# Expert rows fetched by an indirect transfer per pair, and a context branch paced behind the experts' matmuls

## The chip, the cores and the metric

The kernel runs on one core of a Trainium2 chip. A core has a matrix engine (TensorE, PE in the profile; PEld is its weight load), a vector engine (DVE), an activation engine (ACT), a general engine (POOL) and a queue engine (SP) that here only issues transfers. ACT and POOL can issue transfers too. All transfers share the core's 16 DMA engines. The metric is device time in microseconds (us) of one launch.

## The reference, cut to what matters

Two transformer blocks follow one another on 512 tokens of width 1024, all in float32. The first ends in a mixture of experts where each expert chooses its tokens:

```python
def expert_choice_ffn(h, w_router, w_gate, w_up, w_down):
    cap = EC_FACTOR * N // N_EXPERTS                      # 64 tokens for each of 16 experts
    aff = jax.nn.softmax((h @ w_router).astype(F32), axis=-1)
    gate, idx = lax.top_k(jnp.swapaxes(aff, 1, 2), cap)
    xg = jax.vmap(lambda hb, ib: hb[ib])(h, idx)          # the rows that an expert chose
    hid = jax.nn.silu(einsum(xg, w_gate)) * einsum(xg, w_up)   # 64 x 2048
    y = einsum(hid, w_down) * gate[..., None]
    # y is added back into the rows it came from
```

`h` is the normalised token row times one vector plus another (the modulation). One expert's three weight matrices are 1024 x 2048 float32, 25.2 MB; sixteen are 403 MB, most of what the kernel reads. The second block needs, beside its own token stream, the keys, values and scan states of 256 context rows. These depend on inputs alone, so this context branch can run at any time before the second block's mixer.

## The kernel before, in words

A tile framework orders the instructions of each engine; program order and priorities decide, and semaphores are put in by the framework. Three stages matter here.

The router stage (`g_b0`, `g_b1`) normalises the 512 rows into `xn` (four tiles of 128 rows, L1482, L1484), transposes them, computes the router's scores, and finds each expert's 64 tokens. Its result is `slt` (L1574): for each token and expert the slot from 0 to 63, or a number that is no slot.

The expert stage (`g_b`) goes over 16 experts in pairs. At the start of a pair, `pair` builds a 0/1 matrix `S` (512 tokens by 2 x 64 slots, L1589) on DVE and multiplies: for each of 8 slices of the width, 4 matmuls of 128 x 128 with the strided columns of `xn` as weights pick the chosen rows, already transposed; DVE and ACT then apply the modulation on the way out of the accumulator (L1600, L1598) and write `XG`. The first four slices come before the expert's matmuls, the last four after half of its gate and up weights. POOL multiplies `S` by the router's weights (L1602), and four transposes (L1605) make the scatter matrix `P`.

An expert's weights come as 12 tiles of 2 MB ("weight tiles"): 8 alternating between gate and up, then 4 of down. Each is used by 8 matmuls of 64 x 512, which the profile shows as 16 instructions. After the 8 gate and up tiles ACT and DVE form the hidden rows (L1673, L1674), 8 transposes turn them (L1680), and the down tiles follow. After the second expert of a pair, 8 matmuls of 128 x 512 with `P` add its rows into the accumulator `acc` (L1715 to L1718).

Weight tiles land in rooms of 2 MB, and a load is issued by SP, in order, as soon as its room is free, so the matmuls' use of a tile releases a later load. Four rooms go round in a ring (`wr`); three others (`sum_b`, `out_b`, `in_b`) serve once each at the start, before they get their later use. `out_b` later holds the pair's result rows `Y`, `in_b` holds `XG` of every other pair among others. When the context branch has ended, its room makes three more, and the ring has seven.

The context branch (`g_c0`) is a generator: 24 blocks of weights of `w_in_2` (0.5 MB each, 0.25 MB the first), each multiplied with the 256 context rows in 8 matmuls (16 instructions) into the one accumulator `bank_c`, followed by a short convolution on ACT and DVE, transposes and state products. In the expert stage `weave` interleaves it with the experts by weights: an expert counts 0.12, a block of the branch 0.03, and the branch starts at 0.3. The framework may place its matmuls anywhere between those of the experts. Its loads are issued by ACT.

## Time and profile before

| what | value |
|---|---|
| median of 3 runs | 3045.6 us (3041.74 to 3050.76) |
| the profiled execution | 3043.58 us, its span 3041.8 us |
| PE busy in the span | 2863.8 us (94%) |
| DVE, ACT, POOL busy | 1344.8, 911.3, 632.5 us |
| granted TensorE clock, mean | 0.987 |
| moved by DMA | 652.04 MB, mean 214 GB/s |

The profile cuts the span into 40 slices of 76 us. The expert stage is the stretch where the DMA engines are busiest, from about 730 us to 1776 us. There, a table by stretches shows whether PE, the transfers or both are at their limit, and the chain of waits shows what each stretch hung on. A busy PE isn't necessarily PE at its peak: an instruction that streams behind another counts as busy.

### The profile page before, as it was taken

How to read it: one execution, taken by the hardware profiler on the slowest of the kernel's cores; microseconds unless marked ns; L12 is line 12 of the kernel's file. 1: busy time of each engine (PE TensorE's matmuls, PEld its weight loads, DVE VectorE, ACT ScalarE, POOL GpSimd, SP SyncE). 2: the span in 40 equal slices, each digit the busy share in tenths (PEclk: the TensorE clock that was granted, in tenths of full speed). 3: DMA queues.
4: the chain of work that ended last, by engine and by line, in shares of the span. 5: the costliest groups of instructions: out<-in, count | busy, mean ns of one | idle time of the engine just before them, and what ended most of it. 6: DMA issues, size and time to landing. Idle time of an engine off the chain costs nothing.

```text
span 3041.8 us, 42842 instructions
## 1 busy us (share of the span) xinstructions
PE 2863.8 (94%) x17300; PEld 1885.2 (62%) x17300; DVE 1344.8 (44%) x2673; ACT 911.3 (30%) x1855; POOL 632.5 (21%) x662
## 2 busy tenths in 40 slices
PE   7999999998999999899999989999989999999998
PEld 4894557756354534243343348687868678878886
DVE  5522546654221211011011047969797945364445
ACT  5511226532111010000000034545454543243333
POOL 3121225521000000000000022323232323242232
PEclk9999999999999999999999989999999999999999
DMA  7216661047979897999999953333332375243331
GB/s 263 76 45 199 216 195 34 25 162 289 375 310 386 316 371 317 423 430 431 430 431 431 430 192 103 108 87 102 87 115 74 96 261 166 90 153 97 97 104 56
DMA packets 255430, 652.04 MB, mean 214 GB/s; under 512 B 15672, under 2 KB 168760, under 8 KB 230656
## 3 DMA queue, kind: packets, MB, share of 16 engines
q1 hardware_dynamic: 212368, 600.95, 52.5%
q10 hardware_dynamic: 42864, 48.35, 4.8%
q8 instruction: 136, 2.23, 0.3%
q14 instruction: 62, 0.51, 0.1%
HBM read 627.61 MB, written 21.64 MB: 213 GB/s over the span
## 4 chain that ended last, share of the span: by engine, by line
PE 59%; DVE 9%; DMA 5%; ACT 2%; issue 1%; POOL 1%; POOLq 0%; ACTq 0%; DVEq 0%
PE bank_mm L367 25%; PE bigbank L367 22%; PE bank_pj L367 6%; PE bank_c L367 3%; DMA b<-in_w_down 2%; DVE base L2389 1%; PE bank_sm L367 1%; DMA l<-in_w_up 1%; DMA wo<-in_w_down 1%; DVE mix L2393 1%; DVE mix L2392 1%; DMA l<-in_w_gate 1%; PE bank_mm L2144 1%; DVE c L1927 1%; DVE base L2122 1%
## 5 line engine op out<-in xcount | busy, mean ns | idle before, releaser
L367 PE MATMUL bank_pj<-c,c 128*128 128x512 f32 (+2 forms) x1368 | 318.5, 375 | 0.3 <-DVE c L1927 0.3
L367 PE MATMUL bank_mm<-c,c 128*128 128x512 f32 (+1 forms) x1608 | 305.0, 348 | 2.5 <-DVE c L1927 1.3
L367 PEld LDWEIGHTS bank_mm<-c,c 128*128 128x128 f32 x1608 | 259.9, 191 | 42.1 <-DVE c L1927 1.7
L367 PEld LDWEIGHTS bank_pj<-c,c 128*128 128x128 f32 (+1 forms) x1368 | 224.9, 188 | 50.5 <-issue 17.5
L367 PE MATMUL bank_mm<-l 128*128 128x128 f32 (+3 forms) x944 | 227.4, 496 | 4.2 <-DVE l L395 2.0
L1926 ACT CAST c<-base 128x1024 fp32r<-128x1024 f32 x147 | 153.0, 1045 | 253.8 <-PE bigbank L367 105.7
L1927 POOL TENSOR_TENSOR c<-base,c 128x1024 fp32r<-128x1024 f32 x47 | 115.7, 2462 | 450.4 <-DMA base<-in_w_in 201.4
L367 PEld LDWEIGHTS bank_mm<-l 128*128 128x128 f32 (+2 forms) x944 | 155.3, 245 | 73.9 <-issue 65.2
L367 PE MATMUL bigbank<-l 128*64 128x512 f32 (+1 forms) x864 | 195.9, 587 | 4.5 <-DMA l<-in_w_up 2.4
L1927 DVE TENSOR_TENSOR c<-base,c 128x1024 fp32r<-128x1024 f32 x100 | 135.3, 1355 | 139.1 <-ACT c L1926 135.4
L1674 DVE TENSOR_TENSOR b<-l,bigbank 128x512 f32<-128x512 f32 x32 | 20.6, 684 | 257.8 <-PE bigbank L367 227.8
L367 PEld LDWEIGHTS bigbank<-l 128*64 128x64 f32 (+1 forms) x864 | 61.4, 141 | 117.8 <-issue 104.0
L367 PE MATMUL bank_c<-b 128*128 128x256 f32 (+3 forms) x496 | 117.5, 380 | 12.7 <-ACT b L1841 8.3
L1602 POOL TENSOR_TENSOR l<-l,ab 128x512 f32<-128x512 f32 x8 | 8.4, 1048 | 560.2 <-DVE l L1589 506.6
L367 PE MATMUL bigbank<-out,c 128*128 128x512 f32 x480 | 112.5, 394 | 2.4 <-ACT out L2487 1.8
L367 PEld LDWEIGHTS bank_c<-b 128*128 128x128 f32 (+1 forms) x496 | 79.0, 190 | 54.8 <-issue 30.1
L367 PE MATMUL bank_mm<-h,sp 128*128 128x512 f32 (+3 forms) x544 | 106.9, 384 | 4.6 <-ACT h L606 3.8
L367 PEld LDWEIGHTS bank_dn<-dn 64*64 64x64 f32 x1920 | 74.5, 134 | 55.1 <-issue 40.1
L367 PE MATMUL bigbank<-b,l 128*64 128x512 f32 x480 | 105.7, 593 | 2.1 <-DMA b<-in_w_up 1.2
L367 PEld LDWEIGHTS bigbank<-out,c 128*128 128x128 f32 x480 | 90.9, 190 | 22.9 <-ACT out L2487 2.0
L1598 ACT ACTIVATE l<-bank_mm,ab,ab 128x128 f32<-128x128 f32 x32 | 14.7, 458 | 293.0 <-DVE l L1600 292.9
L367 PE MATMUL bigbank<-c,ffn 128*128 128x512 f32 x432 | 100.4, 390 | 0.0
(556 smaller groups left out, 5096.1 us busy)
## 6 DMA issues: line engine op xcount, KB each, us to landing
l<-in_w_up SPq DMA_DIRECT2D x25, 2048.0 KB, 10.7
l<-in_w_gate SPq DMA_DIRECT2D x25, 2048.0 KB, 9.4
l<-in_w_down SPq DMA_DIRECT2D x25, 2048.0 KB, 16.2
base<-in_w_in SPq DMA_DIRECT2D x90, 512.0 KB, 3.7
mods<-in_w_mod SPq DMA_DIRECT2D x80, 512.0 KB, 4.7
base<-in_w_up SPq DMA_DIRECT2D x18, 2048.0 KB, 8.7
wo<-in_w_gate SPq DMA_DIRECT2D x18, 2048.0 KB, 10.2
b<-in_w_gate SPq DMA_DIRECT2D x15, 2048.0 KB, 19.5
```

The costliest lines, as they stand in the source:

```text
L367: self.mm_ins = self.nc.tensor.matmul(out, l, r, start=start, stop=stop).ins
L1598: nc.scalar.activation(XG[:, kt], b[:, kk], AF.Identity, bias=b2[:, kt:kt + 1], scale=a2[:, kt:kt + 1])
L1602: nc.gpsimd.tensor_mul(sc, S, aff[:, :, ee, None].to_broadcast([128, 4, 2, 64]))
L1674: nc.vector.tensor_mul(hid[:, 512 * j:512 * j + 512], s, ac[1][:, j])
L1926: nc.scalar.copy(hi, raw)
L1927: (nc.vector if self.wn % 4 in self.losplit else nc.gpsimd).tensor_sub(lo, raw, hi.bitcast(F32))
L2122: nc.vector.tensor_reduce(mx, s[:, s0:768], AX.X, OP.max)
L2144: nc.tensor.transpose(tb[:, z], p[:, 128 * (g0 + z):128 * (g0 + z) + 128], self.ident)
L2389: nc.vector.scalar_tensor_tensor(E[:, h], rw[:, h, 0], gc(1, 0, h), E[:, h], op0=OP.subtract, op1=OP.min)
L2392: nc.vector.tensor_scalar(W[:, h], cb[:, c, 0], gc(0, 0, h), None, op0=OP.mult)
L2393: nc.vector.scalar_tensor_tensor(W[:, h], cb[:, c, 1], gc(0, 1, h), W[:, h], op0=OP.mult, op1=OP.add)
```

## The change

The rows of `xn` are now written to memory (`xnd`, four transfers of 512 KB issued by ACT in the router stage), and a column `tid` holds each token's row number. For each pair, 4 matmuls of `S` with `tid` (128 x 1) give the row numbers of the 128 slots, DVE converts them to integers, and POOL issues one indirect transfer that fetches the 128 rows (512 KB) into `Y`, the buffer in which the pair's results will stand later. Eight transposes of `Y` then take the place of the 32 matmuls. The modulation and `P` are as before.

The order changes too. The first pair is fetched and transposed before its matmuls. Every later pair is prepared in the odd expert ahead of it: fetch at its start, transposes after its hidden rows, and then the multiplication for `P`. The addition into `acc` is put off into the next expert, half behind its first two weight tiles and half behind its next two.

The room of `xn` becomes a fifth room of the ring (eight after the context branch), and `out_b` no longer serves as a weight room at the start.

The context branch starts at 0.1 instead of 0.3, its steps count 1.7 times as much, an expert's weight is handed out in smaller steps, and each step's PE instructions are ordered behind the last expert matmul issued so far (`issue_after`, which orders instructions on one engine and makes no semaphore). It asks for its weight blocks one block earlier.

```diff
+def paced(K, gen, f):
+    while True:
+        with K.tc.issue_after(K.ex_ins):
+            v = next(gen, None)
+        if v is None:
+            return
+        yield v * f
...
+C0_LATE, C0_PACE = 0.1, 1.7
...
+        z, self.tid = self.small()[:, :1], Part(self.s1b, 144, [4]).ap()
+        nc.vector.tensor_reduce(z, self.km("gt"), AX.X, OP.add)
+        nc.vector.tensor_scalar(self.tid, self.col("iota64", 0, 4), 128.0, z, op0=OP.mult, op1=OP.add)
+        self.xnd = self.dram_tile([512, 1024], "xnorm")
+        for t in range(4):
+            nc.scalar.dma_start(self.xnd[128 * t:128 * t + 128], xn[:, t])
...
-    def pair(self, pr):
+    def pair(self, pr, Y):
...
+        b = self.bank((128, 1))
+        for t in range(4):
+            self.mm(b, S[:, t].rearrange("p e s -> p (e s)"), self.tid[:, t:t + 1], t == 0, t == 3)
+        ix = self.ix[:, pr:pr + 1]
+        nc.vector.tensor_copy(ix, b)
+        nc.gpsimd.indirect_dma_start(Y, None, self.xnd, bass.IndirectOffsetOnAxis(ix, 0))
+        yield
         for k4 in range(2):
             b = self.bank((128, 4, 128))
             for kk in range(4):
-                for t in range(4):
-                    self.mm(b[:, kk], xn[:, t, 4 * k4 + kk::8], S[:, t].rearrange("p e s -> p (e s)"), t == 0, t == 3)
+                nc.tensor.transpose(b[:, kk], Y[:, 4 * k4 + kk::8], self.ident)
...
     def g_b(self, experts=range(16)):
+        self.xn_b.free()
...
-        wr.b += [self.slot(), self.wo_b]
-        more = [None, None, sum_b.ap(), out_b.ap(), None, None, in_b.ap()]
+        wr.b += [self.slot(), self.wo_b, Buf(M, [4096])]
+        more = [None, None, sum_b.ap(), None, None, None, in_b.ap()]
...
+            if e == ex[0]:
+                begun = self.pair(e // 2, yr())
+                next(begun)
+                next(begun)
+            if e % 2 == 0:
+                XG, P, Y = self.nxt
...
-            if e % 2 == 0:
-                Y = yr()
-                prep = self.pair(e // 2)
+            if e % 2 and e != ex[-1]:
+                prep = self.pair(e // 2 + 1, yr())
                 next(prep)
...
+                self.ex_ins = self.mm_ins
+                if owed:
+                    owed.pop(0)()
+                yield 0.018
...
+            with self.tc.issue_after(self.ex_ins):
+                next(prep, None)
+            yield 0.006
...
+                owed += [lambda add=add: add((0, 1)), lambda add=add: add((2, 3))]
+            yield 0.024
...
-            w = wr()
-            self.c0_ld(w, w2[:, :, K0 + 128 * c:K0 + 128 * c + 128])
+            w = block()
...
-            weave(self.g_b(), late(0.3, c0))
+            weave(self.g_b(), late(C0_LATE, paced(self, c0, C0_PACE)))
```

In the rows of the order that follow, `x4` behind a row counts like instructions of the program in a row (a matmul counts once there and as two instructions in the profile). `bigbank` is the accumulator of gate and up, `bank_mm` that of everything else of the experts, `bank_c` that of the context branch; `l_105`, `b_6410`, `base_95` and `wo_6154` are pools of memory, `ab_126` holds the small constants, `base_59` the identity.

PE at the start of the first pair, before:

```order
L1572 MATMUL bank_mm<-base_59,l_105 128x16 x4
L367 MATMUL bank_mm<-l_105 128x128 x19
L367 MATMUL bigbank<-l_105 64x512 x16
L367 MATMUL bigbank<-b_6410,l_105 64x512 x16
L367 MATMUL bank_mm<-l_105 128x128 x13
L367 MATMUL bank_c_7244<-b_6410 128x256 x2
L367 MATMUL bigbank<-base_95,l_105 64x512 x8
```

The same place in the changed kernel:

```order
L1590 MATMUL bank_mm<-base_59,l_105 128x16 x4
L377 MATMUL bank_mm<-ab_126,l_105 128x1 x4
L1618 MATMUL bank_mm<-base_59,b_6410 128x128 x8
L377 MATMUL bigbank<-l_105 64x512 x16
L377 MATMUL bigbank<-b_6410,l_105 64x512 x8
L377 MATMUL bigbank<-base_95,l_105 64x512 x8
L377 MATMUL bigbank<-wo_6154,l_105 64x512 x8
L377 MATMUL bigbank<-l_105 64x512 x24
L1630 MATMUL bank_mm<-base_59,l_105 128x128 x4
L1718 MATMUL bank_mm<-base_59,b_6410 128x128 x8
```

The 19 and 13 picking matmuls are gone. The row numbers (128x1) and the transposes of the fetched rows (L1618) stand one behind the other, with nothing of the context branch between them.

PE from the second to the third expert, where the second pair starts, before:

```order
L367 MATMUL bank_mm<-l_105 64x512 x8
L367 MATMUL bank_c_7543<-b_6410 128x256 x2
L367 MATMUL bank_mm<-b_6410 128x512 x8
L367 MATMUL bank_mm<-l_105 128x128 x19
L367 MATMUL bigbank<-l_105 64x512 x8
```

In the changed kernel the second pair is prepared inside the second expert. Its row numbers, at that expert's start:

```order
L377 MATMUL bank_c_6899<-b_6410 128x256 x8
L377 MATMUL bank_mm<-ab_126,l_105 128x1 x4
L377 MATMUL bigbank<-l_105 64x512 x3
L1899 MATMUL bank_c_6913<-base_59,b_6410 128x128 x2
L377 MATMUL bigbank<-l_105 64x512 x13
L377 MATMUL bigbank<-base_95,l_105 64x512 x8
L377 MATMUL bigbank<-wo_6154,l_105 64x512 x8
L377 MATMUL bank_c_6968<-b_6410 128x256 x8
```

and the transposes of its rows, behind the eighth weight tile:

```order
L377 MATMUL bigbank<-l_105 64x512 x19
L377 MATMUL bigbank<-base_95,l_105 64x512 x8
L1618 MATMUL bank_mm<-base_59,b_6410 128x128 x8
L1718 MATMUL bank_mm<-base_59,b_6410 128x128 x8
L377 MATMUL bank_mm<-wo_6154,l_105 64x512 x8
```

Between the row numbers and the transposes stand the 64 matmuls of eight weight tiles and one block of the context branch; in every later pair it is eleven tiles. A block of the branch is now 8 matmuls in one piece. In the whole stage 19 blocks are left for the expert pairs in both kernels: before, all of them stand in the first three pairs; now 3, 5, 5, 4 and 2 of them in the first five.

POOL from the first pair on, before (L1602 makes `P`'s factor, L1846 and L1857 belong to the context branch):

```order
L1602 TENSOR_TENSOR l_105<-l_105,ab_126 128x512 x2
L1846 TENSOR_TENSOR b_6410<-b_6410 128x512 x2
L1602 TENSOR_TENSOR l_105<-l_105,ab_126 128x512
L1846 TENSOR_TENSOR b_6410<-b_6410 128x512
L1857 TENSOR_TENSOR b_6410<-b_6410 128x512
```

and in the changed kernel (L1613 is the fetch, L1626 and L1905 are L1602 and L1846 of before):

```order
L1613 DMA b_6410<-xnorm,ab_126 128x1024
L1626 TENSOR_TENSOR l_105<-l_105,ab_126 128x512 x2
L1613 DMA b_6410<-xnorm,ab_126 128x1024
L1626 TENSOR_TENSOR l_105<-l_105,ab_126 128x512
L1905 TENSOR_TENSOR b_6410<-b_6410 128x512 x2
L1613 DMA b_6410<-xnorm,ab_126 128x1024
```

The fetches stand in POOL's queue between the multiplications of the context branch, so from the third on a fetch is issued only after those ahead of it.

## Rows read from the trace of the kernel before

**Rows 1.** Page, slices of the whole span: mean GB/s in each of 40.

```profile
GB/s 263 76 45 199 216 195 34 25 162 289 375 310 386 316 371 317 423 430 431 430 431 431 430 192 103 108 87 102 87 115 74 96 261 166 90 153 97 97 104 56
```

**Rows 2.** Chain of waits, pairs' starts and the stage's end: start us, us, what.

```profile
729.99 9.49 PE bank_mm L367 x38
...
868.89 15.78 PE bank_mm L367 x54
...
1026.77 15.78 PE bank_mm L367 x54
...
1180.31 16.04 PE bank_mm L367 x54
...
1306.81 16.05 PE bank_mm L367 x54
...
1776.17 4.66 DMA base<-in_w_in
```

**Rows 3.** Stretches by pair: us, engines' busy us, PEclk, DMA share, GB/s.

```profile
730.00:870.00 140.00, 132.83 (x589) 65.38 (x590) 25.86 (x68) 19.98 (x41) 4.14 (x4) 0.97 0.88 351
870.00:1027.00 157.00, 149.39 (x631) 70.88 (x630) 28.75 (x55) 19.35 (x39) 11.30 (x11) 1.00 0.90 350
1027.00:1180.00 153.00, 145.51 (x608) 67.24 (x606) 24.90 (x47) 16.35 (x34) 13.34 (x13) 0.99 0.86 334
...
1307.00:1424.00 117.00, 109.36 (x485) 47.74 (x485) 15.69 (x28) 5.17 (x10) 1.05 (x1) 1.00 1.01 431
```

**Rows 4.** The same stretches, instructions on the context branch's accumulator alone.

```profile
730.00:870.00 140.00, 29.47 (x118) 20.03 (x118) 5.97 (x14) 5.89 (x17) 0.97 0.88 351
870.00:1027.00 157.00, 41.66 (x148) 24.71 (x148) 10.46 (x20) 9.92 (x20) 1.00 0.90 350
1027.00:1180.00 153.00, 35.60 (x124) 20.59 (x124) 8.53 (x16) 8.42 (x17) 0.99 0.86 334
```

**Rows 5.** Groups by form, 1310 to 1430 us: busy us, mean ns, idle before.

```profile
L367 PE MATMUL bank_mm<-l 128*128 128x128 f32 x64 | 15.5, 401 | 0.0
...
L1598 ACT ACTIVATE l<-bank_mm,ab,ab 128x128 f32<-128x128 f32 x4 | 1.8, 458 | 53.7 <-DVE l L1600 53.7
L1600 DVE TENSOR_SCALAR l<-bank_mm,ab,ab 128x128 f32<-128x128 f32 x4 | 1.6, 407 | 7.5 <-PE bank_mm L367 7.0 <-ACT l L1598 0.5
...
L1605 PE MATMUL bank_mm<-base,l 128*128 128x128 f32 x4 | 0.6, 272 | 0.0
```

**Rows 6.** Chain of waits in a later pair, around one expert's hidden rows.

```profile
1343.63 10.54 PE bigbank L367 x48
...
1360.42 13.95 PE bank_mm L367 x64
1374.37 17.19 PE bigbank L367 x80
```

**Rows 7.** Instructions by time at the first pair: start us, us, engine, idle before.

```profile
729.54 0.29 DVE L1589 TENSOR_TENSOR l<-ab,ab 128x128 f32<-128x128 f32 x1
...
730.74 0.49 DVE L1589 TENSOR_TENSOR l<-ab,ab 128x128 f32<-128x128 f32 x2
...
739.40 7.09 PE L367 MATMUL bigbank<-l 128*64 128x512 f32 x32
...
743.10 0.33 SPq L398 DMA_DIRECT2D l<-in_w_up  x1
...
753.29 6.46 PE L367 MATMUL bank_mm<-l 128*128 128x128 f32 x26
...
764.03 3.60 PE L367 MATMUL bigbank<-wo,l 128*64 128x512 f32 x16
```

**Rows 8.** Transfers of the context branch's blocks (512 KB), 680 to 1200 us.

```profile
DMA to landing us min/median/max: 3.6/4.6/19.8
```

**Rows 9.** POOL's waits, 740 to 1180 us: us in total, times, longest.

```profile
POOL b L1846 <- ACT b L1841: 119.9, 4, 72.0
```

More of the change, by code (lines that the diff above doesn't have):

```diff
@@ L1600, in pair @@
                     nc.vector.tensor_scalar(XG[:, kt], b[:, kk], a2[:, kt:kt + 1], b2[:, kt:kt + 1], op0=OP.mult, op1=OP.add)
-            yield
+        yield
         nc.gpsimd.tensor_mul(sc, S, aff[:, :, ee, None].to_broadcast([128, 4, 2, 64]))
+        yield
         b = self.bank((128, 4, 128))
@@ L1615, in g_b @@
         self.S = Buf(M, [4, 2, 64]).ap()
+        self.ix = Part(self.s1b, 128, [16]).ap().bitcast(mybir.dt.uint32)
         self.XG_r = R(Buf(M, [8, 128]), Part(in_b, 0, [8, 128]))
@@ L1636, in fetch @@
                 self.ld(w, src)
-        gt2, ex = self.gt2_b.ap(), list(experts)
+        gt2, ex, owed = self.gt2_b.ap(), list(experts), []
         self.fg_b = self.gt1_b
         for e in experts:
-            if not self.c0 and len(wr.b) < 7:
+            if not self.c0 and len(wr.b) < 8:
                 p = wr.i % len(wr.b)
@@ L1657, in g_b @@
             for q in range(4):
-                if q == 2:
-                    next(prep, None)
                 for m, src in enumerate((g, u)):
@@ L1667, in g_b @@
                                 self.mm(ac[m][64 * a:64 * a + 64, j], XG[:, kt, 64 * (e % 2):64 * (e % 2) + 64], w[:, k2, 1024 * a + 512 * j:1024 * a + 512 * j + 512], kt == 0, kt == 7)
-            for _ in prep:
-                pass
+                self.ex_ins = self.mm_ins
+                if owed:
+                    owed.pop(0)()
+                yield 0.018
+            if e == ex[0]:
+                for _ in begun:
+                    pass
             hid = hr()
@@ L1690, in g_b @@
                             self.mm(dn[64 * h:64 * h + 64], hT[:, 4 * q + j, 64 * a:64 * a + 64], w[:, j, 512 * h:512 * h + 512], a + q + j == 0, a == 1 and q == 1 and j == 3)
+                self.ex_ins = self.mm_ins
+                next(prep, None)
+                if a == 0:
+                    yield 0.018
             pp = slice(64 * (e % 2), 64 * (e % 2) + 64)
@@ L1704, in g_b, with add @@
                 self.c_open()
-            if e % 2:
                 for t in range(4):
-                    if e == ex[-1]:
-                        b = on.pop(0) if on else under(t)
-                        for h in range(2):
-                            hs = slice(512 * h, 512 * h + 512)
-                            self.mm(b[:, hs], P[:, 128 * t:128 * t + 128], Y[:, hs], False, True)
-                        self.c_tile(t, b)
-                        continue
-                    for h in range(2):
-                        b = self.bank()
-                        self.mm(b, P[:, 128 * t:128 * t + 128], Y[:, 512 * h:512 * h + 512])
-                        o = acc[:, t, 512 * h:512 * h + 512]
-                        nc.vector.tensor_add(o, o, b)
-            yield 0.12
+                    b = on.pop(0) if on else under(t)
+                    for h in range(2):
+                        hs = slice(512 * h, 512 * h + 512)
+                        self.mm(b[:, hs], P[:, 128 * t:128 * t + 128], Y[:, hs], False, True)
+                    self.c_tile(t, b)
+            elif e % 2:
+                def add(ts, P=P, Y=Y):
+                    for t in ts:
+                        for h in range(2):
+                            b = self.bank()
+                            self.mm(b, P[:, 128 * t:128 * t + 128], Y[:, 512 * h:512 * h + 512])
+                            o = acc[:, t, 512 * h:512 * h + 512]
+                            nc.vector.tensor_add(o, o, b)
+                owed += [lambda add=add: add((0, 1)), lambda add=add: add((2, 3))]
+            yield 0.024
 BF = mybir.dt.bfloat16
@@ L1791, in g_c0, with ask, block @@
         w2 = self.w2()
-        w = wr()
-        self.c0_ld(w[:, :, :64], w2[:, :, DT0:DT0 + 64])
+        cols = [(DT0, 64)] + [(K0 + 128 * c, 128) for c in range(4)]
+        for gr in range(4):
+            cols += [(XS0 + 512 * gr + 128 * i, 128) for i in range(4)] + [(BM0 + 128 * gr, 128)]
+        asked = []
+        def ask():
+            if cols:
+                o, n = cols.pop(0)
+                asked.append(wr())
+                self.c0_ld(asked[-1][:, :, :n], w2[:, :, o:o + n])
+        def block():
+            ask()
+            return asked.pop(0)
+        ask()
+        w = block()
         b = self.bank((128, 256), "c0")
@@ L1800, in g_c0 @@
         for c in range(4):
-            w = wr()
-            self.c0_ld(w, w2[:, :, K0 + 128 * c:K0 + 128 * c + 128])
+            w = block()
             for t in range(2):
@@ L1866, in g_c0 @@
                 ch = (XS0 + 512 * gr + 128 * i) if i < 4 else (BM0 + 128 * gr)
-                w = wr()
-                self.c0_ld(w, w2[:, :, ch:ch + 128])
+                w = block()
                 b = self.bank((128, 256), "c0")
```

5 lines of the change are left out of this document (2 added, 3 removed).

## Prediction

> **What bounds the kernel now.** I read the page's slices first, then the chain of waits inside the expert stage, then the stretches by pair, and last the rows of single steps. The slices show two halves of the stage [rows 1]: from the tenth to the sixteenth slice the transfers move 289 to 386 GB/s, after that 423 to 431 GB/s without a break. The chain gives the pairs' starts [rows 2]: 730.0, 868.9, 1026.8, 1180.3 and 1306.8 us, and the stage's end at 1776.2 us. So the first four pairs take 138.9, 157.9, 153.5 and 126.5 us, and the last four 469.4 us, 117.3 each.
>
> What limits a late pair? Its 24 weight tiles of 2.097 MB are 50.3 MB, which at 431 GB/s [rows 3] is 116.8 us (4.87 us a tile). That is the pair's length: late pairs hang on the transfers. PE is nearly full beside them. By the chain [rows 6] an expert's gate and up matmuls end at 1354.2 us, its down matmuls start at 1360.4 us and end at 1374.4 us, and this first expert of the pair had begun at 1306.8 us: 67.6 us without a wait for a load. The second one, taken without waits, is 8 tiles of 3.6 us [rows 7], the 6.2 us between, and 13.95 us: 49.0 us. Together PE needs 116.6 us, as much as the transfers.
>
> What limits an early pair? PE is busy 132.8 of 140, 149.4 of 157 and 145.5 of 153 us there, and the transfers run at 334 to 351 GB/s [rows 3]. The instructions on the context branch's accumulator hold PE for 29.5, 41.7 and 35.6 us of it [rows 4]. So in the first three pairs the context branch stands on top of a PE that was full already, and the transfers lose what PE is late. The fourth pair (126.5 us) has no branch left but runs on four rooms.
>
> The gain therefore lies in the first four pairs, where PE time counts. In the last four a shorter PE buys nothing.
>
> **The change part by part.** All numbers are us, against the profiled execution (3043.58, of which the span is 3041.8). The median of the runs, 3045.6, is 2.0 more; I subtract the same gain from it.
>
> *Picking matmuls out.* 64 instructions, 15.5 a pair [rows 5]. On the path in pairs one to four; hidden under the transfers later.
>
> *Row numbers, transposes in.* The 4 narrow matmuls are 8 instructions. No row shows this form. The same count of transposes would take 1.2 (0.15 each, 0.6 for four [rows 5]), of picking matmuls 1.9 (0.242 each). I take 1.5, in the middle. The 8 transposes are 1.2. The drains of the transposes to `XG` are as many as before, 4 on ACT at 0.458 and 4 on DVE at 0.407 [rows 5], but they now stand in front of the copies of the turned hidden rows, which the down tiles wait for: 1.6. Sum 4.3 a pair, on the path in the first four pairs (bounds 2.4, with nothing behind the drains, and 4.7). Net 15.5 - 4.3 = 11.2 a pair.
>
> *The fetch.* For later pairs PE has other work between the row numbers and the transposes. In the second pair it is eight tiles and a block of the branch, 8 x 3.6 + 5.6 = 34; in the others eleven tiles, at least 39. A 512 KB transfer lands in 4.6, at most 19.8 [rows 8]. So I cost the wait at nothing there. The first pair has no cover: `S` is complete at 731.2 [rows 7], the row numbers 1.5 later at most, the conversion 0.3 (as the nearest small DVE row, a part of `S`, takes 0.29), landing 4.6, about 2.4 more since a weight tile of 4.87 is under way at that time (half of it), transposes 1.2, first drain 0.4. First expert matmul at 741.6 instead of 739.4 [rows 7]: +2.2. With the landing at 3.6 alone or at 19.8 this is -1 to +15. In return the second half of the old picking, 6.5 at 753.3 [rows 7], goes, and the first half is what the fetch replaces.
>
> DVE is busy 28.8 of 157 us in an early pair, in 55 instructions of 0.5 us [rows 3]; what that does to a transfer that POOL issues, no row shows. The Trainium skill, page "SBUF — State Buffer", section "A bandwidth-pool intuition that's wrong", speaks against such a fetch: POOL writes the descriptors itself and waits while a vector copy holds the port that the two share; it gives 0.62 us for a transfer alone and 3.1 us beside such a copy. By that rule I estimate up to 2.5 us more at the first pair and nothing under the cover, and the sum would come to 2998 or 2999.
>
> *Rows of xn to memory.* Four issues on ACT in front of the drains that feed the router, and two small DVE instructions: no row for their delay in that place; each issue of a transfer on a queue takes some 0.33 [rows 7]. Four are 1.3; I take +1.5 for all (0 to 3).
>
> *The branch spread.* 19 blocks cost 29.5 + 41.7 + 35.6 = 106.8 before, 5.6 each. Now 3, 5, 5, 4 and 2 of them stand in pairs one to five: 16.8, 28, 28, 22.4, 11.2. That changes pairs one to three by -12.7, -13.7 and -7.6, and loads the next two.
>
> *Weight rooms.* Five instead of four while the branch runs, one fewer at the start. Pairs two and three need 24 x 4.87 + 5 x 1.2 + 1.2 = 124 of transfers, PE more than that, so I give the fifth room no gain of its own.
>
> The sum by pairs:
> - first: 138.9 + 2.2 - 6.5 + 4.3 (preparing the second) - 12.7 = 126.2
> - second: 157.9 - 11.2 - 13.7 = 133.0
> - third: 153.5 - 11.2 - 7.6 = 134.7
> - fourth: PE 116.6 - 11.2 + 22.4 = 127.8 (transfers 122.9)
> - fifth: PE 116.6 - 11.2 + 11.2 = 116.6, transfers 116.8 + 2.4 + 1.2 = 120.4; the transfers end last
> - sixth and seventh: 116.8 + 1.2 (the fetch's 0.5 MB) = 118 each; eighth 117.3
>
> Together 995.4 instead of 1046.2: 50.8 less. Minus 1.5 for the stores: 49.3. The profiled execution would take 2994 and the median 2996.
>
> What is late next: PE in the first four pairs, still, and the transfers from the fifth on. Two things I leave at zero, since they pull against each other: rooms that are full when the branch ends give a lead of at most 3 tiles (15 less), and pairs two to four run both limits within 10 us of each other, where each hiccup of one stalls the other (a few us a pair more).
>
> **The rivals.**
>
> *The transfers never idle (2958, chance 0.15).* If blocks fill the 6.2 us pauses at the hidden rows [rows 6], PE keeps up everywhere. From the eighth load at 743.1 [rows 7] there are 185 tiles (900), 19 blocks (23), 4.9 for `acc`, 7 fetches (8.5), 4.9 of states: 941, and a last tile's 3.6, so 1688 instead of 1776.2: 88 less. For it: in the changed order a block stands in the pause of some experts. Against it: PE's sum in pairs two and three is 9 above the transfers'.
>
> *The solid blocks stall PE (3021, chance 0.22).* The branch has one accumulator. Its transposes now come a few expert matmuls behind a block (half a tile, 1.8 us), and must wait until ACT and DVE have drained the block and convolved it: three passes of about 0.5 each [rows 4] and their hand-overs. Where that takes 3 us instead of 1.8, 19 blocks lose 1.3 each: 25 of the 49 are gone. For it: PE executes in order, so an expert's ready matmul stands behind. Against it: DVE and ACT are busy under 20% [rows 3].
>
> *The fetch comes late (3100, chance 0.05; the slower side).* From the third fetch on it stands in POOL's queue behind multiplications of the branch, which waited up to 72 us for their turn before [rows 9]. PE's transposes wait in order, and all expert matmuls and releases of rooms behind them. The cover is 34 in the second pair and about 50 in the next three (11 tiles and two blocks). At 72 us that is 38 + 3 x 22 = 104 against the 49 gained: 55 slower, 3100. It turns from gain to loss at about 58 us. Against it: those multiplications belong to blocks that are earlier in PE's order too.
>
> *Nothing moves (3045, chance 0.06).* The transfers themselves would have to be slow in the first pairs, and not PE late. Their 334 to 351 GB/s beside a PE at 95% speak against it [rows 3].
>
> **How the numbers follow.** My forecast has 0.52, the four rivals 0.15, 0.22, 0.05 and 0.06. The likeliest time is 2996. The unknown terms (start -1 to +15, stores 0 to 3, the drains -2, lead and stalls about 15 to each side) make 2976 to 3019 for it alone. Out to most of the two neighbouring rivals the range is 2964 to 3027. 0.3% is 9 us, about what a measurement here can tell from no change: faster has 0.52 + 0.15 + 0.21 = 0.88 (a little of the second rival falls short), same 0.06 + 0.01 = 0.07, slower 0.05.
>
> **What would show it.** Right: pairs of about 126, 133, 135, 128 and then 117 to 120; no matmul group of 15.5 us at a pair's start; first expert matmul within some us of 742; the branch's last instruction near the end of the fifth pair; transfers near 400 GB/s in pairs two to four. Wrong: PE waiting at L1618 in later pairs (fetch late); PE waiting at L1899 for DVE (solid blocks); transfers at 431 from the second pair on (first rival); pairs six to eight below 116.

## The result and the profile after

| | before | changed |
|---|---|---|
| median | 3048.2 us | 2996.95 us (2990.4 to 3003.8, 4 runs) |
| ratio | 1 | 0.9839 (95%: 0.9806 to 0.9872) |
| profiled execution | 3043.58 us | 2990.43 us, its span 2988.6 us |

One run of the kernel before took 4054 us; the median above counts it, the ratio leaves it out. The forecast was 2996 us. How did it come about, and is it the time that the forecast was made of?

The page's slices of the changed kernel, mean GB/s in each of 40, answer [rows 1]:

```profile
GB/s 268 75 36 198 219 209 30 37 148 278 412 416 414 395 416 412 410 382 431 429 431 431 428 98 102 121 70 128 64 122 68 125 250 158 93 158 93 98 99 57
```

From the eleventh slice on the transfers now move 382 to 416 GB/s, where it was 310 to 386 up to the sixteenth. They still don't reach 431 until the nineteenth slice.

The stretches by pair answer [rows 3]. Columns: stretch, us, busy us (and instructions) of PE, weight loads, DVE, ACT and POOL, granted clock as a share of full speed, DMA share, GB/s.

```profile
727.00:846.00 119.00, 108.02 (x496) 45.24 (x496) 23.72 (x68) 16.51 (x30) 5.34 (x5) 0.96 0.93 383
846.00:976.00 130.00, 122.86 (x527) 49.33 (x528) 21.68 (x45) 15.55 (x34) 7.15 (x7) 0.99 0.99 414
976.00:1109.00 133.00, 124.22 (x534) 49.88 (x533) 23.05 (x46) 12.85 (x27) 8.20 (x8) 1.00 0.98 405
1109.00:1239.00 130.00, 124.69 (x534) 50.10 (x534) 22.74 (x44) 13.42 (x28) 8.20 (x8) 1.00 0.98 405
1239.00:1369.00 130.00, 118.40 (x488) 43.62 (x486) 19.37 (x36) 10.31 (x21) 9.20 (x9) 0.99 0.95 403
1369.00:1487.00 118.00, 99.13 (x438) 33.02 (x436) 15.23 (x28) 4.96 (x10) 2.03 (x2) 1.00 1.01 430
```

The reader is to see two things. PE's time fell in the first three pairs and in the late ones (109 to 99), and rose in the fourth and fifth, which now hold blocks (112 to 125 and 109 to 118); but only the first three pairs became shorter. And in pairs two to four the DMA engines are busy for 0.98 to 0.99 of the time, at 405 to 414 GB/s, while PE has 5 to 9 us of idle time.

A pair's length is taken from the first instruction that weights a pair's last results (DVE, line 1734, before 1692) to the same of the next pair. The first pair counts from the first instruction that picks rows, at 729.99 us before and 727.17 after. All in us:

| pair | 1 | 2 | 3 | 4 | 5 | 6 | 7 | 8 | sum |
|---|---|---|---|---|---|---|---|---|---|
| before | 137.9 | 157.4 | 154.3 | 126.5 | 116.7 | 117.8 | 117.0 | 118.5 | 1046.2 |
| forecast | 126.2 | 133.0 | 134.7 | 127.8 | 120.4 | 118 | 118 | 117.3 | 995.4 |
| changed | 118.5 | 129.9 | 133.4 | 130.5 | 130.0 | 117.9 | 119.2 | 117.8 | 997.2 |

The expert stage gave 49.0 of the 53.2 us between the two profiled executions. Of the rest, 2.8 came before it and 1.3 after it.

The chain of waits from the second to the fourth pair (start us, us, what; the longest of 157 pieces) answers [rows 2]:

```profile
by line: DMA b<-in_w_in 31.0%; PE bigbank L377 23.2%; PE bank_mm L377 17.0%; DMA l<-in_w_up 15.0%; PE bank_c L377 10.8%; DVE b L1709 0.7%; SPq L408 0.6%; ACT l L403 0.6%; PE bank_c L1899 0.6%; PE bank_mm L1718 0.6%; PE bank_mm L1630 0.4%; P
...
838.17 33.96 DMA b<-in_w_in
872.62 13.30 DMA l<-in_w_up
893.37 29.35 DMA b<-in_w_in
923.67 17.03 DMA l<-in_w_up
```

`b<-in_w_in` is a branch's weight block, 512 KB. Its landing takes up to 34 us, where it was 3.6 to 19.8 before [rows 8]; some blocks still land within 3.5 to 10 us. 46% of this chain are transfers. What do they hold up? SP's waits in the same stretch (us in total, times, longest):

```profile
SPq L408 <- PE bigbank L377: 157.8, 39, 9.8
SPq L408 <- DMA b<-in_w_in: 143.7, 8, 20.4
```

Eight times SP, which issues the experts' weights, waits for the landing of a branch's block. It needs nothing of that block, which goes into a room of the branch. Why the program makes it wait isn't in the trace. After one of these waits, at 872 us, SP issues three loads within 3 us.

The first pair by time (start us, us, engine, line, operation, idle before) answers [rows 7]:

```profile
726.73 0.29 DVE L1607 TENSOR_TENSOR l<-ab,ab 128x128 f32<-128x128 f32 x1
...
728.26 0.61 PE L377 MATMUL bank_mm<-ab,l 128*128 128x1 f32 x4 [0.21 <-DVE l L1607]
728.90 0.16 DVE L1612 CAST ab<-bank_mm 128x1 uint32<-128x1 f32 x1 [0.49 <-PE bank_mm L377]
...
729.93 1.21 POOL L1613 DMA_INDIRECT b<-xnorm,ab  x1 [12.05 <-issue]
...
736.66 1.97 PE L1618 MATMUL bank_mm<-base,b 128*128 128x128 f32 x8 [7.79 <-DMA b<-xnorm,ab]
...
738.56 2.79 PE L377 MATMUL bigbank<-l 128*64 128x512 f32 x8
```

And all eight fetches (durations of the POOL instruction in ns, min/median/max; its transfers' landing in us; who waited for line 1613):

```profile
L1613 POOL DMA_INDIRECT b<-xnorm,ab x8: 980/983/1213, 729.9 to 1534.1; - x8
...
  PE bank_mm L1618: 7.8, 1
...
DMA to landing us min/median/max: 6.3/11.0/11.4
```

From `S` to the first expert matmul it takes 11.83 us instead of 9.86. PE waits for a fetch once, in the first pair.

### The profile page after: what moved, and what is told of

It reads as the page before. It is cut to its first block, busy times and chain, and to the rows that moved or that the text cites. A ratio compares the mean times of both kernels' runs of the same rounds, so it can differ in the third digit from the quotient of the medians.

```text
span 2988.6 us, 42066 instructions
## 1 busy us (share of the span) xinstructions
PE 2780.2 (93%) x16916; PEld 1779.9 (60%) x16916; DVE 1342.4 (45%) x2683; ACT 910.4 (30%) x1855; POOL 641.8 (21%) x670
## 4 chain that ended last, share of the span: by engine, by line
PE 46%; DMA 17%; DVE 8%; issue 2%; ACT 1%; POOL 1%; SPq 0%; POOLq 0%; ACTq 0%; DVEq 0%
PE bank_mm L377 18%; PE bigbank L377 17%; DMA l<-in_w_up 7%; PE bank_pj L377 6%; DMA l<-in_w_down 4%; DMA b<-in_w_in 4%; PE bank_c L377 2%; DMA l<-in_w_gate 1%; DVE base L2447 1%; PE bank_sm L377 1%; DVE mix L2451 1%; DVE mix L2450 1%; DVE c L1985 1%; PE bank_mm L2202 1%; DVE base L2180 1%
## 5 line engine op out<-in xcount | busy, mean ns | idle before, releaser
L377 PE MATMUL bigbank<-l 128*64 128x512 f32 (+1 forms) x1104 | 264.0, 593 | 25.4 <-DMA l<-in_w_up 19.1
L377 PEld LDWEIGHTS bigbank<-l 128*64 128x64 f32 (+1 forms) x1104 | 78.2, 140 | 185.4 <-issue 139.8
L1708 ACT ACTIVATE l<-bigbank 128x512 f32<-128x512 f32 x32 | 17.4, 594 | 420.4 <-PE bigbank L377 420.4
L377 PE MATMUL bank_mm<-l 128*64 128x512 f32 (+2 forms) x528 | 125.1, 598 | 11.2 <-DMA l<-in_w_down 9.3
L1803 ACT ACTIVATE b<-bank_c,base 128x256 f32<-128x256 f32 x20 | 11.3, 564 | 307.0 <-PE bank_c L377 307.0
L377 PE MATMUL bigbank<-b,l 128*64 128x512 f32 x352 | 82.5, 607 | 19.8 <-DMA b<-in_w_gate 11.2
L377 PE MATMUL bank_dn<-dn 64*64 64x64 f32 x1920 | 96.2, 225 | 4.2 <-DVE dn L988 1.3
```

Of the source, the lines that this page charges most:

```text
L377: self.mm_ins = self.nc.tensor.matmul(out, l, r, start=start, stop=stop).ins
L1708: nc.scalar.activation(s, ac[0][:, j], AF.Silu)
L1803: nc.scalar.activation(y, b, AF.Identity, scale=wc(1), bias=self.col(bname, i))
```

## The experiments

Two theories were set against each other. T is the prediction: PE bounds pairs one to four. R came from the rows above: the transfers bound pairs two to five, slowed by the branch's loads. Each result is a ratio to the kernel before in the same series (median 3046 to 3048 us), mostly of five runs. The last column is the sum of pairs two to four in the profiled execution, in us (393.8 in the first one of the changed kernel).

| kernel | median us | ratio (95%) | pairs 2 to 4 |
|---|---|---|---|
| changed, again | 2997.7 | 0.9838 (0.9824 to 0.9851) | 399.1 |
| fetch alone | 3010.4 | 0.9872 (0.9856 to 0.9887) | 399.5 |
| spread alone | 3042.6 | 0.9988 (0.9979 to 0.9997) | 420.3 |
| four rooms | 3002.4 | 0.9854 (0.9839 to 0.9869) | 388.3 |
| branch's loads out | 2982.1 | 0.9791 (0.9777 to 0.9805) | 376.3 |
| branch's products out | 2996.8 | 0.9835 (0.9821 to 0.9849) | 396.3 |
| both out | 2948.3 | 0.9682 (0.9668 to 0.9696) | 357.1 |
| 1 KB pieces | 3001.6 | 0.9849 (0.9835 to 0.9863) | 391.0 |
| rooms later | 2990.4 | 0.9815 (0.9802 to 0.9828) | 397.2 |
| rooms later, slower pace | 2996.8 | 0.9849 (0.9835 to 0.9864) | 395.0 |
| rooms later, blocks on SP | 2977.6 | 0.9782 (0.9767 to 0.9797) | 381.9 |
| the same, products out | 2973.9 | 0.9766 (0.9753 to 0.9780) | 379.5 |

### The measure

No edit.

> The changed kernel once more, as the measure for the three kernels that share its runs. Every theory: 2997 us, within 0.3%; pairs of 118, 130, 133, 130, 130, 118, 119, 118 us.

The time came again, 2997.7 us. The profiled execution's third pair took 142.0 us at a granted clock of 0.95, the others within 4 us of the first profile. So a single pair of a single profile can be off by 9 us. What follows rests on medians and on sums over pairs; where a single pair is named, this reserve holds unless several profiles agree on it.

### Each half alone

```diff
-            weave(self.g_b(), late(C0_LATE, paced(self, c0, C0_PACE)))
+            weave(self.g_b(), late(0.3, c0))
```

> The changed kernel with the branch woven in as before (a share of 0.3 later, no pace, not held behind each expert's matmuls); fetch, five rooms and the new order of a pair's steps stay. T (the prediction: PE limits pairs one to four, the branch's blocks simply stand in it): pair one 118 + 12.7 = 131, pairs two and three before's 157 and 154 minus 11.2 = 146 and 143, pair four without blocks 118 (transfers), the rest 118 each: 1010 against 997, so about 3009 us. R (the transfers limit pairs two to five, whose cost is that of the blocks' loads wherever they stand): the sum of the pairs stays within 3 us of 997, 2997 us.

3010.4 us: T's number, and R's is refuted for this kernel. Pair by pair T was less exact: the second took 153.5 and the third 130.6 us, where it had 146 and 143. The second pair (stretch, us, busy us of the engines as above) is PE's, which waits for no transfer there:

```profile
866.00:1020.00 154.00, 144.66 (x614) 62.77 (x613) 29.34 (x58) 19.06 (x41) 11.19 (x11) 0.99 0.97 376
```

Where the blocks stand bunched (47 us of the branch in this pair), PE is the bound. The fetch alone gives 38 of the 50 us; this kernel also keeps the fifth room and the new order of a pair's steps.

```diff
-        b = self.bank((128, 1))
-        for t in range(4):
-            self.mm(b, S[:, t]..., self.tid[:, t:t + 1], t == 0, t == 3)
-        ix = self.ix[:, pr:pr + 1]
-        nc.vector.tensor_copy(ix, b)
-        nc.gpsimd.indirect_dma_start(Y, None, self.xnd, bass.IndirectOffsetOnAxis(ix, 0))
         yield
+        xn = self.xn_b.ap()
...
-                nc.tensor.transpose(b[:, kk], Y[:, 4 * k4 + kk::8], self.ident)
+                for t in range(4):
+                    self.mm(b[:, kk], xn[:, t, 4 * k4 + kk::8], S[:, t]..., t == 0, t == 3)
...
```

The rows of `xn` stay in their room, so this kernel has four rooms, and seven after the branch.

> The other half of the change alone: the branch held behind each expert's matmuls and the new order of a pair's steps, but the rows picked by 64 matmuls a pair as before, with xn kept in the room's place (four rooms). The kernel with the fetch alone took 3010 us. If the parts add (before 3046: fetch 36 less, spread 13 less): 3035 us. If the picking matmuls, 11.2 us a pair net, are on the path only in the first four pairs (prediction): 3002 us of the changed kernel with four rooms, plus 4 x 11.2 less the 8 us by which PE is short of the transfers there in three of them: 3002 + 45 - 15 = about 3032 us, and pairs six to eight stay at 118. If the fetch were what makes the spread pay: 3046 us or more.

3042.6 us: the spread alone gives 4 us, less than two of the three expectations had, and next to the third (none, the fetch makes the spread pay). By pairs not even that is the spread's: the first five take 8.9 us more than before (701.7 against 692.8), and the gain comes from the eighth, which took 105.7 where 118 was expected. The picking matmuls stand on the path in five pairs and not in four, since the spread puts blocks into the fifth pair too. The fourth and the fifth pair of this kernel:

```profile
1147.00:1291.00 144.00, 138.32 (x587) 63.94 (x583) 23.77 (x44) 13.06 (x27) 7.23 (x7) 1.00 0.91 370
1291.00:1432.00 141.00, 130.82 (x539) 58.38 (x538) 19.81 (x36) 11.01 (x22) 9.28 (x9) 0.99 0.93 390
```

Here PE is nearly full in every pair with blocks, and a block moved is a block paid for. The parts don't add: 38 and 4 alone, 50 together. The spread pays 13 once the fetch has made room on PE. And against the next kernel, which has the same four rooms and differs from this one by the fetch, the fetch is worth 40 us; the forecast had 4 x 11.2 = 45.

### Four rooms

```diff
-        wr.b += [self.slot(), self.wo_b, Buf(M, [4096])]
+        wr.b += [self.slot(), self.wo_b]
...
-            if not self.c0 and len(wr.b) < 8:
+            if not self.c0 and len(wr.b) < 7:
```

> The changed kernel without the fifth room: four rooms while the branch runs, seven later. T (the prediction gave the fifth room nothing): 2997 us within 0.3%, pairs two to four 130 to 133. Rival: the fifth room is what keeps the transfers at a share of 0.98 while SP's loads wait behind the branch's blocks (waits of up to 20 us in the trace, four tiles): then the share falls to 0.93 or less in pairs two to four, about 6 us a pair, and the time is 3012 us or more.

4.7 us slower, with intervals that overlap: T's 2997 within 0.3% holds. The rival's 3012 doesn't, and the DMA share didn't fall in pairs two to four (1.00, 1.00, 0.98), so the rival is refuted. The first pair is 126.3 us instead of 118.5 and the second 126.0 instead of 129.9. That would fit one more tile that comes early with the fifth room, half of which the second pair gives back; the trace wasn't followed further.

### Which limit holds pairs two to four

```diff
-                self.c0_ld(asked[-1][:, :, :n], w2[:, :, o:o + n])
+                if len(self.c0_lds) < 7:
+                    self.c0_ld(asked[-1][:, :, :n], w2[:, :, o:o + n])
```

> The changed kernel without the loads of the branch's weight blocks after the seventh (left out: some 18 loads of 512 KB; the branch computes on with the columns that stand in its three buffers). All its matmuls stay. T (PE limits pairs one to four; a block's transfer was 1.2 us beside it): at most the fifth pair moves, 2990 to 2997 us; pairs two to four stay at 130 to 133. R (transfers limit pairs two to five, at 405 to 414 GB/s): 50.3 MB at 430 GB/s is 117, so these pairs come down to their PE time: 123 to 125 busy in two to four, 118 in five: 7 + 9 + 6 + 10 = about 30 us less, 2967 us.

```diff
-                for kt in range(8):
-                    self.mm(b, w[:, kt], hc[:, kt], kt == 0, kt == 7)
+                self.mm(b, w[:, 0], hc[:, 0])
```

> The changed kernel with one of the eight matmuls of each XS and BM block of the branch (left out: seven eighths of its 20 products); its loads, drains, convolutions and transposes stay. That takes 4.9 us a block off PE, 93 us in all. T (PE limits pairs one to four, transfers would need 124): 6 to 9 us off each of pairs two to four, about 20 less, 2977 us. R (transfers limit pairs two to five): these pairs stay at 130 within 3; PE only shows more idle time; 2990 to 2997 us.

Both edits in one kernel:

> Both at once: the branch's later loads and seven eighths of its products left out. Either theory: nothing but 50.3 MB and 0.5 MB of rows a pair, so all eight pairs at 118 or 119 (first 112 or more): 12 + 15 + 12 + 11 = 50 us less than the changed kernel, 2947 us. If a pair stays above 122, a third thing (SP's waits, the drains in front of the hidden rows' copies) holds it.

The third pair of each. First the loads out, then the products out, then both:

```profile
970.00:1098.00 128.00, 124.69 (x534) 50.58 (x532) 22.98 (x45) 12.93 (x27) 8.20 (x8) 0.99 0.98 411
```

```profile
976.00:1109.00 133.00, 112.82 (x464) 37.60 (x463) 22.78 (x45) 12.86 (x27) 8.21 (x8) 0.97 0.98 405
```

```profile
960.00:1082.00 122.00, 109.89 (x464) 37.76 (x462) 22.61 (x45) 12.86 (x27) 8.21 (x8) 0.99 1.01 430
```

Products out: 57 us of PE are gone from the branch's instructions (99 to 42; the 93 expected had taken a block's whole 5.6 for its products), and the time moves by 1. Not all of the 57 was a relief: the mean granted clock of pairs two to four was 0.94 to 0.97 of full speed, with PE idle for 14 to 20 us in each, where the changed kernel had 0.99 to 1.00, and PE's busy time in the first five pairs fell by 40. Even so PE waited more: its weight loads waited 48 us for the experts' tiles in pairs two to four, against 23 in the changed kernel. The largest entry of each, the changed kernel first:

```profile
PEld bigbank L377 <- DMA l<-in_w_up: 12.8, 5, 3.4
```

```profile
PEld bigbank L377 <- DMA wo<-in_w_up: 10.1, 3, 5.5
```

That settles R for the changed kernel: the transfers bind. Loads out: 15 us less, half of what R expected and more than T allowed. PE comes next, only 4 to 9 us a pair behind, and no weight load waits for a tile any more. The DMA share of its third pair is 0.98 all the same, so a share near 1 alone doesn't show that the transfers bind. The fifth pair stays at 129.9, so its length isn't the loads' doing. Both out: 49 us less, as both theories had it. Two pairs stay above the 122 that was named as the sign of a third limit: the third at 122.6, which ran at 430 GB/s throughout, so it is the transfers', and the fifth at 123.8, where SP stood 25 us at a new room (see below). So two limits stand side by side, and taking away either alone shows less than both.

The price of a block's load follows from the last two. With PE out of the way, pairs two to four take 396.3 us with the 13 loads and 357.1 without: 39.2, or 3.0 each. That is a difference of two single profiles, the first at the lower clock just named and the second at 0.99 to 1.00, so it is rough.

### Larger pieces

```diff
-        wr.b += [self.slot(), self.wo_b, Buf(M, [4096])]
+        wr.b += [self.slot(), self.wo_b]
+        wide = Buf(M, [4096])
+        self.wide = [Part(wide, 2048 * i, [8, 256]) for i in range(2)]
...
+                if self.wide and o < BM0 and (o - XS0) % 256 == 0:
+                    cols.pop(0)
+                    z = self.wide[0].ap()
+                    self.wide = self.wide[::-1]
+                    self.c0_ld(z, w2[:, :, o:o + 256])
+                    asked.extend([z[:, :, :128], z[:, :, 128:]])
+                    return
...
```

> The changed kernel with the fifth room's memory given to the branch: its XS columns come 256 at a time, in pieces of 1 KB instead of 512 bytes, two blocks to a load; four rooms for the experts until the branch ends, eight after. T (transfers don't limit pairs two to four, the fifth room is worth nothing): no change, 2997 us. R (the transfers' rate sets these pairs, and the short pieces lower it): with the same MB at 420 instead of 408 GB/s pairs two to five lose 3 to 4 us each, down towards PE's 123 to 125: 2984 us, if four rooms do; if four rooms are too few, as much more as e2 shows.

No gain: it stands with the four rooms (3001.6 against 3002.4 us). R's 3 to 4 us a pair didn't come. SP's waits for the branch's landings fell, to 66.5 us from 95.5 with the four rooms, and the time didn't: so these waits don't by themselves set the time. Its loads by time to landing (KB each, median us), and SP's waits:

```profile
l<-in_w_in ACTq DMA_DIRECT2D x4, 1024.0 KB, 34.1
```

```profile
SPq L408 <- DMA l<-in_w_in: 66.5, 5, 17.2
```

1 MB in pieces of 1 KB lands in 34.1 us, as 512 KB in pieces of 512 bytes did at the longest (33.96 in the chain above). Both are 1024 pieces, 64 on each of 16 engines. So the longest landings go with the number of pieces and not with the bytes. Blocks that landed in 3.5 to 10 us had the same number of pieces, so what else is under way counts too.

### The rooms of the branch's memory

SP and then PE in the fifth pair of the changed kernel, by time:

```profile
1287.25 0.42 SPq L408 DMA_DIRECT2D l<-in_w_up  x1
1312.52 0.33 SPq L408 DMA_DIRECT2D b<-in_w_up  x1
1313.02 0.33 SPq L408 DMA_DIRECT2D b<-in_w_gate  x1
```

```profile
1320.19 5.35 PE L377 MATMUL bigbank<-b,l 128*64 128x512 f32 x16 [4.64 <-DMA b<-in_w_up]
```

The three new rooms are put next in line when the branch's program ends, but its last states are still being worked on. SP stands 25 us at the first of them.

```diff
-            if not self.c0 and len(wr.b) < 8:
+            ended += not self.c0
+            if ended > 1 and len(wr.b) < 8:
```

> The changed kernel with the three rooms from the branch's memory added one expert later. In the trace of the changed kernel SP stands from 1287 to 1313 us at a load into such a room, until the branch's last state is copied out, and the fifth pair takes 130 us where the sum had 120.4. If that wait is the 9.6 us: the fifth pair falls to 120 or 121 and the time to 2988 us. If the fifth pair is long because its blocks' loads cost as much as in pairs two to four: it stays near 130, 2997 us. If five rooms are too few for the expert in between: 3000 us or more.

2990.4 us, and the fifth pair took 120.0 us, at 430 GB/s: the first reading, and the forecast's 120.4 for that pair. The five kernels above that have the changed kernel's paced branch with all its products took 129.8 to 130.0 there.

### One queue instead of two

```diff
-        self.c0_eng = self.nc.scalar
```

> The kernel with the rooms one expert later, and besides the branch's weight blocks are loaded by SP's queue, in line with the experts' weights, instead of ACT's. So far: with the products of the branch left out pairs two to four kept 128 to 135 us at 402 to 410 GB/s, with its loads left out they fell to 121, 129 and 127, so the transfers bind there, and 13 blocks cost 39 us more than none (3.0 each against the prediction's 1.2). Theory Q: most of the excess comes from the two queues side by side: a block's 64 packets of 512 bytes on each engine take turns with packets of 14.6 KB (0.54 us each at 27 GB/s), which is the landing of up to 34 us, and SP's next loads wait for that landing. In one queue a block costs about 2 us: pairs two to four fall to the level of the kernel without the loads, 121 to 129, and the time from 2990 to about 2976 us; landings of 34 us are gone. Theory W: the short pieces cost the same wherever they stand: 2990 us within 0.3%. Theory S: a block's load waits in SP's line for its buffer and holds the weights behind it: 2996 us or more.

2977.6 us, Q's number. The line had moved the branch's loads to ACT's queue at the start of the expert stage. Without it they stay in SP's. The second to fourth pair:

```profile
848.00:972.00 124.00, 121.06 (x527) 49.59 (x527) 21.88 (x45) 15.56 (x34) 7.17 (x7) 1.00 1.01 422
972.00:1100.00 128.00, 124.70 (x534) 50.65 (x532) 22.82 (x45) 12.95 (x27) 8.21 (x8) 1.00 1.02 425
1100.00:1230.00 130.00, 127.97 (x536) 51.53 (x534) 22.62 (x44) 13.43 (x28) 8.21 (x8) 0.99 1.01 423
```

The same loads, now at 422 to 425 GB/s with SP no longer waiting for a landing of the branch (its five largest waits are all for PE). The chain of this stretch is PE's:

```profile
by line: PE bigbank L377 45.4%; PE bank_mm L377 32.4%; PE bank_c L377 15.7%; PE bank_c L1900 1.4%; DVE b L1710 1.0%; PE bank_mm L1719 0.8%; PE bank_mm L1630 0.4%; ACT l L403 0.4%; PE bank_mm L1618 0.4%; DVE l L405 0.4%; DVE b L1735 0.3%; AC
```

To separate the price from PE, the last run took the products out of this kernel too (with the edit shown above):

> The kernel with the rooms later and the branch's blocks in SP's queue, and one of the eight matmuls of each XS and BM block (left out: seven eighths of their products). This gives the price of a block's load in one queue with PE out of the way. With both left out pairs two to four took 116.5 + 122.6 + 118.0 = 357 us, with the loads on ACT's queue 396. Theory Q (the excess comes from two queues side by side): 13 or 14 blocks at 1.2 to 1.9 us, so 373 to 383, and 2960 to 2972 us in all. Theory W (short pieces cost 3.0 each wherever they stand, and the gain of the run before came from elsewhere): 396 or at best the 382 of that run, 2977 us or more.

Pairs two to four take 379.5 us: 22.4 above 357.1, or 1.6 for each of the 14 loads that fall there (1.7 over 13) against 3.0 with two queues. The time, 2973.9 us, lies 2 above Q's range. So the second queue accounts for 17 of the 39 us. Of the other 22, 16 to 17 are the blocks' bytes at 431 GB/s (1.2 each), and some 6 are left for the short pieces. The clock differed here too (0.97 to 0.99 in this profile). With the products in, at 0.99 to 1.00 in both, moving the blocks to SP's queue takes pairs two to four from 397.2 to 381.9 us, 15 less, and PE's weight loads wait 1.6 us for transfers there instead of 26.

Is it the turns between the queues, as Q says? In the changed kernel's stretch from 846 to 1239 us the profile has these queues (packets, MB, share of 16 engines' time; q1 is SP's, q10 ACT's):

```profile
q1 hardware_dynamic: 10291, 149.98, 90.4%
q10 hardware_dynamic: 15159, 8.59, 7.0%
```

A packet of q1 is 14.6 KB on average. At 27 GB/s an engine (430 over 16) that is an estimate of 0.54 us, and 64 turns of one for one are 34.6 us: the longest landing. The Trainium skill, page "DMA: Bandwidth & Descriptors", section "Queues, rings and completion order", says that a DMA engine serves its queues in turn, a packet at a time. The landings of 34 us at 512 bytes and at 1 KB agree, if a turn is a single piece; the page's typical packet of 9 to 17 descriptors would make 4 to 8 turns of it. The turns themselves aren't in the trace. What the runs show is that landing, waits and price go with the second queue.

### A slower pace

```diff
-C0_LATE, C0_PACE = 0.1, 1.7
+C0_LATE, C0_PACE = 0.1, 2.2
```

> The kernel with the rooms one expert later, and the branch spread thinner (pace 2.2 instead of 1.7), so that its last blocks fall into the sixth pair. If PE bound pairs two to four (the prediction), each gets about a block less and loses some 5 us, while late pairs, whose PE has 18 us to spare, take the blocks for 1.2 of transfer each: about 2980 us. If the transfers bind from the second pair on, the blocks cost the same wherever they stand: 2990 us within 0.3%.

On top of the later rooms it is 6 us slower (10 by the ratios). T's 2980 is refuted; the other number, 2990 within 0.3%, holds at its edge. PE is relieved (119.5 and 119.2 busy in pairs three and four instead of 124.7 and 126.3), and these two become only 3 us shorter, while the second is 4 longer and the fifth goes from 120.0 to 133.7. That speaks against T once more. Why a pair with fewer blocks is as long as one with more isn't settled. The trace points to SP's waits: in pairs two to five it waited 148 us for landings on ACT's queue, 72 for blocks and 77 for stored states of the branch, against 144 with the later rooms alone, and PE's weight loads waited 58 us for tiles against 29. No run tested that.

## Why the prediction was right, and where it wasn't

The total was right: 49.0 us from the stage against 50.8. Half of its inner working was not, and that the total came out in spite of it is luck: errors of both signs cancel, as follows.

**What held.** The picking matmuls are worth much in the early pairs and nothing in the late ones: pairs six to eight are at 117.8 to 119.2, though PE has 19 us to spare there. The first expert matmul is 2.0 later by `S`, forecast 2.2, by other parts: the row numbers and their conversion were done 0.7 us after `S` was complete and not 1.8, POOL began the fetch 0.9 later, which the forecast lacked, and the rows landed in 6.7 us (from 729.93 to the transposes), near its 4.6 + 2.4. The cover of the later fetches held: landings of up to 11.4 us, no wait of PE. This refutes the rival of the late fetch. The rival of the stalled blocks is refuted by the waits: in pairs two to four PE waited 0.8 us for DVE at the branch's transposes. The rival without idle transfers came half true: they are busy almost without a pause (0.98 to 0.99), but slower than its 431 GB/s, since it too priced a block at 1.2 us. The branch's PE time came to 99 us instead of 107. It stands in five pairs, but by the pairs as measured the 19 blocks lie 3, 4, 5, 5 and 2, where the forecast had 3, 5, 5, 4 and 2.

**The step that failed: "PE's sum in pairs two and three is 9 above the transfers'".** The forecast had PE at 133 and 134.7 there and the transfers at 124. The kernel without the loads shows what PE needs: 120.9 and 128.6. The kernel without the products shows what the transfers need: 127.8 and 133.5. The order is reversed; summed over pairs two to four, it is 376.3 for PE and 396.3 for the transfers, and the changed kernel's two profiles have 393.8 and 399.1. Two terms were mis-sized, with opposite signs:
- PE's. The length of before's pairs was taken as PE's time, but PE was busy 149.4 of 157 [rows 3], and the difference was carried over. It held no wait for transfers: before, PE's waits there (870 to 1180 us, the two largest below) are mostly for ACT, DVE and POOL at the branch's own steps, 13 us, and the changed kernel has 0.8 of them in pairs two to four. Besides, the branch's instructions held PE for 21.1 and 24.8 us in these two pairs, not 28 each.
- The transfers'. "1.2 us" for a block is its bytes at 431 GB/s. It costs about 3.0 beside a full queue of SP, and 1.6 to 1.7 in the same queue. The forecast put no price on what a block's landing holds up: it knew landings of 3.6 to 19.8 [rows 8], from a stage in which the queues had pauses. The change closed the pauses.

```profile
PE bank_c L367 <- ACT b L1841: 6.5, 11, 1.1
PE bank_c L367 <- ACT b L393: 3.6, 5, 0.8
```

The larger of each pair's two limits came out nearly the same (129.9 and 133.4), and so, by luck, the total did. A forecast for the next step would have failed: it would have cut PE's work in pairs two to four, and that gives 1 us.

**The fifth pair: forecast 120.4, measured 130.0.** The prediction saw in the new rooms only a lead, and left it at zero. They arrive with the branch's end, which the change moved from the third pair into the fifth, and SP waited there. With the rooms an expert later the pair takes 120.0.

**The first pair: forecast 126.2, measured 118.5.** "I give the fifth room no gain of its own": with four rooms the pair takes 126.3, and 122.9 in the kernel with 1 KB pieces, which has four as well; with five it took 118.5 and 120.3. So that term was some 5 to 8 off in this pair, of which the second pair gives a part back; over the whole it is 4.7, hardly clear of the noise. This and the fifth pair cancel, by luck again.

**Stores and fetch port.** The 1.5 us for the stores, which no row had, can't be told: the stage starts between 726.5 and 733.2 us in the changed kernel and its variants. The Trainium skill, page "SBUF — State Buffer", section "A bandwidth-pool intuition that's wrong", would by the forecast's estimate have put up to 2.5 us on a fetch beside a vector copy. The POOL instruction took 0.98 to 1.21 us in all eight fetches, with no case near the page's 3.1. In the first pair DVE had nothing to do from the fetch's issue to its landing; beside the second fetch it was busy for 1.17 of 1.20 us, with no copy among its instructions, and the POOL instruction took 0.98. So no run here shows the page's case.

**A better version.** With the rooms an expert later and the branch's blocks in SP's queue it takes 2977.6 us, 0.9782 of the kernel before; the changed kernel has 0.9838. In its pairs two to four PE and the transfers both stand at their limit: without the products only 4 us more come off, and a run without the branch's loads on top of it is missing.

## What to carry to other kernels

Where two limits lie within 10 us of each other, a right total proves neither: take each away alone, then both, before deciding what to shorten next. A price read in a stage with pauses (here a transfer's landing) doesn't hold once the change has closed the pauses. And small pieces on a second queue beside a full one can cost more than their bytes: here about 3.0 us a block, and 1.7 in the same queue.

## What the runs showed of the hardware

- The longest landings beside a full queue went with the number of pieces: 512 KB in pieces of 512 bytes up to 33.96 us, 1 MB in pieces of 1 KB 34.1 us, while all transfers together kept 405 to 417 GB/s.
- The same block cost the transfers about 3.0 us from a second queue and 1.6 to 1.7 from the same queue, 1.2 of it for its bytes at 431 GB/s.
- An indirect fetch of 128 rows of 4 KB holds POOL for 0.98 us and lands 6.3 to 11.4 us after its issue.
